# Output projection of a two-layer hybrid decoder trunk: which two mixers are summed first, in what order the projections are made, and how fast the background work is issued

## The chip, the cores and the metric

The kernel runs on one core of one Trainium2 chip. The metric is the device time of one execution in microseconds (us). Before the change it is 1254.05 us, the median of 3 runs (1253.93 to 1257.28).

## The reference

All data is f32; x is 512 tokens by 1024 channels. Each of two layers first makes four mixers of 256 channels out of one projection of the normed x, then sums them through one output projection, and ends with a SwiGLU feed-forward:

```python
for l in range(2):
    mod = silu(c) @ ada_w[l] + ada_b[l]            # six vectors of 1024
    sh1, sc1, g1, sh2, sc2, g2 = split(mod, 6)
    h = rmsnorm(x, norm_mix_g[l]) * (1 + sc1) + sh1
    fq, fk, fv, ff, pu, rq, rk, rv, rg, cu = split(h @ w_in[l])
    y_fox  = fox_attention(fq, fk, fv, ff, fox_fb[l])   # 4 heads x 64, causal, forget gate
    y_pool = pool_mixer(pu, pool_w[l], pool_scale[l])   # running means over 2, 4, 8, 16
    y_ret  = retention(rq, rk, rv, rg, gn_g[l])         # 4 heads x 64, chunks of 128, head norm, gate
    y_conv = conformer_conv(cu, ...)                    # GLU, depthwise k=31, layernorm, swish
    mix = concat([y_fox, y_pool, y_ret, y_conv])
    x = x + g1 * (mix @ w_out[l])
    h = rmsnorm(x, norm_ffn_g[l]) * (1 + sc2) + sh2
    x = x + g2 * ((silu(h @ w1[l]) * (h @ w3[l])) @ w2[l])
return rmsnorm(x, final_g)
```

## The kernel before

Activations lie channel by token: a tile is 128 channels by 512 tokens, so x is eight tiles `xT` and each mixer is two. `mix[0..7]` are, in this order, fox 0 and 1, pool 0 and 1, ret 0 and 1, conv 0 and 1.

**Products.** Every f32 product is three passes of TensorE (PE) over halves of the operands, a rounded part and a rest: L265 rounded by rounded, L266 rest of the data by rounded weight, L267 rounded data by rest of the weight. A weight tile comes by DMA (`raw`, mostly 512 KB), ScalarE (ACT) makes its rounded part `wh` (L164) and VectorE (DVE) the rest `wl` (L169). Activations are split likewise (`ah` L479 on ACT, `al` L480 on DVE; `yh` L438 and `yl` L442 for the normed x). There are 3 PSUM banks `mm` for products, 4 called `sm` and one `aux`, and 4 pairs `wh`/`wl`.

**Background work.** What isn't a big product is written as generators that are advanced a step at a time in `slot()`, which the main code calls after each product; each has a rate (`r_...` in layer 0, `q_...` in layer 1). They are: `ada`/`adaV`, which multiplies the ada_w rows by silu(c) on DVE (L318, L320; here called acs steps; a 256 KB DMA each into 3 buffers `ada`, with a small POOL copy L659 ahead of each load, and a set of 8 steps gives 512 of the 6144 columns); `conv` (30 multiply-adds for each of two tiles at L740, then a tail: column sums on PE L746, L748, squares L751 and L753, L404, L416, the power on POOL L408, back over the partitions L424, L758 to L761, split); `fox` (L812 to L850); `ret` for the pairs of heads 0 and 1 (scores L905, L911, states L922 to L930, sums L939 and L944, then the head norm: ACT L947, PE L951, DVE L416, POOL L408, DVE L957, PE L961, DVE L963, split L479/L480); and `pool` (L983 to L997). `finish_bg` runs a generator to its end at that place of the program. A scheduler may still move instructions of different generators past each other; each engine then works off its own list in order.

**Order of the main code.** After the fox and conv projections come those named in the table `MO`: `pu` (pool), `rk`, `rq`, `rv`, `rg` (gate of retention, L1136 and L1137, whose tile `hp` has 2 buffers that the conv taps also use) and four `o`. An `o` is a quarter of part 1 of the output projection: two of the eight output tiles, over four of the eight mixer tiles, added to `xT` through L1052. Before the change part 1 sums pool and conv. Part 2 sums fox and ret: three tiles with the mixer outermost, in the order `OB`, then five tiles in two halves of 256 tokens. The second norm follows (L404, L408, L424, L429, L438), and then the feed-forward in three segments of 8, 7 and 7 hidden tiles; a gated tile is L1232 on DVE, then L479/L480. During the feed-forward of layer 0 `adaV` makes the last vector of layer 0 and five of layer 1.

## Time and profile before

| | |
|---|---|
| median of 3 runs | 1254.05 us |
| the profiled execution | 1255.27 us |
| its span, first to last instruction | 1253.5 us |
| PE busy | 1209.0 us, 96% |
| DVE busy | 761.2 us, 61% |
| ACT busy | 406.5 us, 32% |
| POOL busy | 95.5 us, 8% |
| mean granted PE clock | 0.974 |
| HBM read | 154.74 MB |

A line of the page's groups gives the line of the kernel, engine and operation, what is written and read, how often, then busy time and mean ns of one, then the idle time of the engine just before. A line of the waits says which engine sat at which line for whom, the sum, how often, and the longest, all in us. A line of the timeline is start and duration, and in brackets idle time before it and what ended that. A line of the windows gives, for a stretch, each engine's busy time (and instructions), the granted PE clock, the DMA share and GB/s.

### The profile page before, as it was taken

What the parts mean: (1) busy time and instruction counts of PE and PEld (TensorE: products, weight loads), DVE (VectorE), ACT (ScalarE), POOL (GpSimd) and SP (SyncE); (2) the same over time, 40 slices, a digit from 0 to 9 for tenths busy, and PEclk for the clock granted to TensorE, in tenths of its full rate; (3) what the DMA queues carried; (4) which work ended last, traced back from release to release, by engine and by line L of the source; (5) the groups of instructions that cost most, each with busy time, mean ns of one, the idle gap of its engine ahead of it and who ended that gap; (6) DMA issues with size and microseconds to landing.
All of it is one profiled execution on the core that took longest, in us unless ns stands there. A gap on an engine that the chain in (4) does not pass through costs nothing.

```text
span 1253.5 us, 16762 instructions
## 1 busy us (share of the span) xinstructions
PE 1209.0 (96%) x6373; PEld 1004.1 (80%) x6373; DVE 761.2 (61%) x1332; ACT 406.5 (32%) x654; POOL 95.5 (8%) x186
## 2 busy tenths in 40 slices
PE   9999989999998999999999999899999999999997
PEld 8778666789876888888899886678988888888887
DVE  6799997577777555453357998457653333333333
ACT  5433334244322222123234244424432223213222
POOL 5432210102000000000000000000100000000000
PEclk8999978999998999999999999899999999999999
DMA  9766622226777545343233343022443323233321
GB/s 308 215 207 187 201 86 76 68 68 190 244 226 239 167 135 173 103 137 97 75 96 95 96 130 84 9 94 84 154 149 101 99 86 99 74 113 101 95 74 68
DMA packets 223721, 160.05 MB, mean 128 GB/s; under 512 B 8374, under 2 KB 198032, under 8 KB 223640
## 3 DMA queue, kind: packets, MB, share of 16 engines
q1 hardware_dynamic: 223464, 158.90, 42.7%
q8 instruction: 50, 0.82, 0.3%
q14 instruction: 31, 0.25, 0.1%
q10 hardware_dynamic: 176, 0.08, 0.0%
HBM read 154.74 MB, written 2.11 MB: 125 GB/s over the span
## 4 chain that ended last, share of the span: by engine, by line
PE 74%; DMA 5%; DVE 4%; issue 1%; ACT 1%; POOL 0%; DVEq 0%; ACTq 0%
PE mm L265 22%; PE mm L266 22%; PE mm L267 22%; DMA ada<-in_ada_w 4%; DVE acs L320 1%; PE sm L812 1%; PE sm L850 1%; PE sm L265 1%; PE sm L266 1%; PE sm L267 1%; DVE wl L169 1%; DMA raw<-in_ffn_w 1%; PE sm L838 1%; PE aux L404 0%; PE sm L961 0%
## 5 line engine op out<-in xcount | busy, mean ns | idle before, releaser
L164 ACT CAST wh<-raw 128x1024 fp32r<-128x1024 f32 (+3 forms) x196 | 198.8, 1015 | 592.4 <-PE mm L266 385.0
L266 PE MATMUL mm<-yl,wh 128*128 128x512 f32 (+1 forms) x984 | 373.1, 381 | 2.2 <-DVE yl L442 2.1
L265 PE MATMUL mm<-yh,wh 128*128 128x512 f32 (+1 forms) x984 | 369.5, 382 | 5.2 <-ACT yh L438 5.2
L267 PE MATMUL mm<-yh,wl 128*128 128x512 f32 (+1 forms) x984 | 372.1, 379 | 0.0
L169 DVE TENSOR_TENSOR wl<-raw,wh 128x1024 fp32r<-128x1024 f32 (+3 forms) x196 | 231.7, 1183 | 137.8 <-ACT wh L164 131.2
L266 PEld LDWEIGHTS mm<-yl,wh 128*128 128x128 f32 x984 | 188.1, 191 | 38.6 <-DVE yl L442 3.5
L265 PEld LDWEIGHTS mm<-yh,wh 128*128 128x128 f32 x984 | 185.4, 191 | 40.6 <-ACT yh L438 6.2
L267 PEld LDWEIGHTS mm<-yh,wl 128*128 128x128 f32 x984 | 188.0, 191 | 36.3 <-issue 0.2
L265 PE MATMUL mm<-ah,wh 128*128 128x512 f32 (+1 forms) x516 | 189.4, 370 | 6.2 <-ACT ah L479 6.2
L266 PE MATMUL mm<-al,wh 128*128 128x512 f32 (+1 forms) x516 | 189.8, 368 | 0.8 <-DVE al L480 0.8
L267 PE MATMUL mm<-ah,wl 128*128 128x512 f32 (+1 forms) x516 | 188.7, 367 | 0.0
L320 DVE SCALAR_TENSOR_TENSOR acs<-ada,cact,acs 128x512 f32<-128x512 f32 x140 | 104.8, 748 | 42.6 <-DMA ada<-in_ada_w 40.4
L1052 DVE SCALAR_TENSOR_TENSOR xT<-mm,mod,xT 128x512 f32<-128x512 f32 (+1 forms) x86 | 57.7, 675 | 117.1 <-PE mm L267 116.8
L265 PEld LDWEIGHTS mm<-ah,wh 128*128 128x128 f32 x516 | 97.3, 189 | 24.0 <-ACT ah L479 6.8
L266 PEld LDWEIGHTS mm<-al,wh 128*128 128x128 f32 x516 | 97.6, 189 | 17.7 <-DVE al L480 1.2
L267 PEld LDWEIGHTS mm<-ah,wl 128*128 128x128 f32 x516 | 97.6, 189 | 17.1 <-issue 0.2
L1232 DVE TENSOR_TENSOR t<-t,mm 128x512 f32<-128x512 f32 x42 | 28.8, 685 | 100.5 <-PE mm L267 100.5
L740 DVE SCALAR_TENSOR_TENSOR hc<-hp,cwT,hc 128x512 f32<-128x512 f32 x120 | 85.3, 745 | 1.0 <-ACT hc L737 0.9
L408 POOL TENSOR_TENSOR r<-r,mhalf 128x2 f32<-128x2 f32 (+3 forms) x16 | 18.1, 1133 | 535.3 <-DVE r L416 535.3
L659 POOL COPY ada<-yl 128x1 f32<-128x1 f32 x80 | 42.0, 531 | 153.7 <-DVE acs L320 103.1
L265 PE MATMUL mm<-wh,yh 128*128 128x256 f32 (+1 forms) x128 | 39.4, 308 | 2.7 <-DVE v L1124 2.7
L438 ACT ACTIVATE yh<-t,mod 128x256 fp32r<-128x256 f32 (+1 forms) x56 | 27.9, 533 | 35.6 <-DVE t L429 27.7
(257 smaller groups left out, 1176.2 us busy)
## 6 DMA issues: line engine op xcount, KB each, us to landing
raw<-in_ffn_w SPq DMA_DIRECT2D x104, 512.0 KB, 4.2
ada<-in_ada_w SPq DMA_DIRECT2D x160, 256.0 KB, 3.4
raw<-in_w_in SPq DMA_DIRECT2D x32, 512.0 KB, 4.2
raw<-in_ffn_w SPq DMA_DIRECT2D x32, 448.0 KB, 3.6
ad<-in_ada_w SPq DMA_DIRECT2D x32, 256.0 KB, 5.9
raw<-in_w_out SPq DMA_DIRECT2D x32, 256.0 KB, 3.1
raw<-in_w_in SPq DMA_DIRECT2D x4, 520.0 KB, 4.4
xn<-in_x SPq DMA_DIRECT2D x4, 512.0 KB, 6.4
```

The lines of the kernel that those rows point to most:

```text
L164: A.copy(h[:, 0:n], raw)
L169: V.tensor_tensor(out=lo[:, 0:n], in0=raw, in1=f(h[:, 0:n]), op=ALU.subtract)
L265: PE.matmul(o, lh, rh, start=start, stop=False)
L266: PE.matmul(o, lh, rl, start=False, stop=False)
L267: PE.matmul(o, ll, rh, start=False, stop=stop)
L320: V.scalar_tensor_tensor(out=acc, in0=r, scalar=ck, in1=acc, op0=ALU.mult, op1=ALU.add)
L408: G.tensor_tensor(out=out_, in0=ms, in1=mhalf[:, 0:ms.shape[-1]], op=ALU.pow)
L438: A.activation(yh[k][:, u:v], y, AF.Identity, bias=shift(l, i, k), scale=1.0)
L659: G.tensor_copy(t_[:, 0:1], f(yl[k][:, at:at + 1]))
L740: V.scalar_tensor_tensor(out=hcs[j], in0=hps[j][:, t:t + S], scalar=cwT[:, l, j, t:t + 1], in1=hcs[j], op0=ALU.mult, op1=ALU.add)
L1052: V.scalar_tensor_tensor(out=xT[:, n, u:v], in0=b[:, u:v], scalar=mod[l][:, gcol + n:gcol + n + 1], in1=xT[:, n, u:v], op0=ALU.mult, op1=A ...
L1232: V.tensor_tensor(out=t_, in0=t_, in1=b3, op=ALU.mult)
```

## The change

Part 1 of the output projection now sums fox and ret (order `OA`: fox 0, ret 0, fox 1, ret 1), part 2 pool and conv. Before part 1 the program finishes retention and fox instead of pool and conv; pool is finished at the first tile of part 2, conv at its third. While part 1 runs, `conv` and `ada` take their rates from a new table `LATE` (2.0 each). In both layers the projections come as `rk rq rv rg pu`, so the gate of retention is made ahead of part 1; layer 1 made it between the third and the fourth `o` before. The rates also change, and `FB` (layer 0) goes from 1 to 2.

```diff
-... 'MO': 'pu rk rq rg rv o o o o', 'MO1': 'pu rk rv rq o o o rg o', ... 'FB': 1, 'FB1': 2, ... 'r_ada': 0.6, 'r_conv': 0.7, 'r_fox': 0.85, ... 'r_adaV': 0.4, 'q_conv': 1, ... 'OA': (1, 0, 2, 3), 'OA1': (0, 1, 3, 2), 'OB': (1, 2, 0, 3), 'OB1': (1, 3, 0, 2), ...
+... 'MO': 'rk rq rv rg pu o o o o', 'MO1': 'rk rq rv rg pu o o o o', ... 'FB': 2, 'FB1': 2, ... 'r_ada': 0.45, 'r_conv': 0.65, 'r_fox': 1.2, ... 'r_adaV': 0.7, 'q_conv': 0.65, ... 'OA': (0, 2, 1, 3), 'OA1': (0, 2, 1, 3), 'OB': (0, 1, 2, 3), 'OB1': (0, 1, 2, 3), ...
+LATE = dict(conv=2.0, ada=2.0)
...
             if n == "o":
-                plan.append(wout(l, outs, 1))
+                plan.append(wout(l, outs, 0))
...
-        plan += [wout(l, i, 0) for i in range(4)]
+        plan += [wout(l, i, 1) for i in range(4)]
...
     def slot(w=1.0):
         for e in list(running):
-            e[1] += RATE[cur["layer"]][e[0]] * w * cur["on"]
+            r = LATE.get(e[0]) if cur["part"] else None
+            e[1] += (r or RATE[cur["layer"]][e[0]]) * w * cur["on"]
...
         def do_o():
             if not outs:
-                finish_bg(pg)
-                finish_bg([cg])
+                finish_bg(rgens)
+                finish_bg([fg])
+                cur["part"] = 1
...
-                    prod_out(b, h, lo, c, q, (2, 3, 6, 7)[q], 0, S, q == qs[0], q == qs[-1])
+                    prod_out(b, h, lo, c, q, (0, 1, 4, 5)[q], 0, S, q == qs[0], q == qs[-1])
...
             if q == 0:
-                finish_bg([fg])
+                finish_bg(pg)
             if q == 2:
-                finish_bg(rgens)
+                finish_bg([cg])
             for i in range(N1):
-                prod_out(banks[i], *tile_of(i), i, q, (0, 1, 4, 5)[q], 0, S, q == qs[0], q == qs[-1])
+                prod_out(banks[i], *tile_of(i), i, q, (2, 3, 6, 7)[q], 0, S, q == qs[0], q == qs[-1])
```

The same exchange of mixer tiles stands in the two loops of part 2 that follow. Line numbers of the changed kernel are higher by 2 to 5 (L740 becomes L743, L320 L323, L1052 L1055, L1232 L1237).

On VectorE in layer 0, the last steps of the second pair of heads (`qk_438` is its tile, `r8` its variances, `xT_93` the residual, `wl` the rest of a weight tile) stood before among evictions of the output projection:

```order
L957 SCALAR_TENSOR_TENSOR qk_438_2334<-sm_426_2259,vecH_120,hp_332_1747 128x512
L1052 SCALAR_TENSOR_TENSOR xT_93<-mm_428_2276,mod0_110,xT_93 128x512
L169 TENSOR_TENSOR wl_431_2294<-raw_429_2289,wh_430_2292 128x1024
L1052 SCALAR_TENSOR_TENSOR xT_93<-mm_435_2312,mod0_110,xT_93 128x512
L416 TENSOR_SCALAR r8_434_2309<-aux_121 128x8
L1052 SCALAR_TENSOR_TENSOR xT_93<-mm_442_2350,mod0_110,xT_93 128x512
L169 TENSOR_TENSOR wl_445_2368<-raw_443_2363,wh_444_2366 128x1024
L963 TENSOR_TENSOR qk_438_2334<-qk_438_2334,sm_439_2336 128x512
L480 TENSOR_TENSOR al_441_2347<-qk_438_2334,ah_440_2346 128x512
```

Now the same steps (`qk_382`) come ahead of every eviction, and the acs steps (`acs_458`) of the adaLN vectors lie between them:

```order
L419 TENSOR_SCALAR r8_377_1996<-aux_121 128x8
L316 TENSOR_TENSOR mod0_110<-aux_121,adbT_118 128x4
L321 TENSOR_SCALAR acs_458_2426<-ada_459_2427,cact_117 128x512
L323 SCALAR_TENSOR_TENSOR acs_458_2426<-ada_460_2431,cact_117,acs_458_2426 128x512
L323 SCALAR_TENSOR_TENSOR acs_458_2426<-ada_461_2444,cact_117,acs_458_2426 128x512
L316 TENSOR_TENSOR mod0_110<-aux_121,adbT_118 128x4
L323 SCALAR_TENSOR_TENSOR acs_458_2426<-ada_462_2448,cact_117,acs_458_2426 128x512
L323 SCALAR_TENSOR_TENSOR acs_458_2426<-ada_463_2452,cact_117,acs_458_2426 128x512
L966 TENSOR_TENSOR qk_382_2021<-qk_382_2021,sm_383_2023 128x512
L323 SCALAR_TENSOR_TENSOR acs_458_2426<-ada_464_2456,cact_117,acs_458_2426 128x512
L323 SCALAR_TENSOR_TENSOR acs_458_2426<-ada_465_2469,cact_117,acs_458_2426 128x512
L483 TENSOR_TENSOR al_385_2034<-qk_382_2021,ah_384_2033 128x512
```

The variance step and the product with it (L416 and L963, now L419 and L966) were two evictions and a weight split apart; now five acs steps lie between them, and two more ahead of the split of the result.

On TensorE in layer 1, the spreading of the head norm (L961; `r8_1301` are its variances) stood before inside a run of output projection products:

```order
L266 MATMUL mm_1311_7385<-al_1118_6393,wh_1272_7170 128x512
L267 MATMUL mm_1311_7385<-ah_1117_6392,wl_1273_7172 128x512
L265 MATMUL mm_1311_7385<-ah_1171_6617,wh_1272_7170 128x512
L266 MATMUL mm_1311_7385<-al_1172_6618,wh_1272_7170 128x512
L961 MATMUL sm_1307_7357<-ident_74,r8_1301_7330 64x128 x8
L267 MATMUL mm_1311_7385<-ah_1171_6617,wl_1273_7172 128x512
L265 MATMUL mm_1311_7385<-ah_1262_7102,wh_1272_7170 128x512
L266 MATMUL mm_1311_7385<-al_1263_7103,wh_1272_7170 128x512
L267 MATMUL mm_1311_7385<-ah_1262_7102,wl_1273_7172 128x512
```

Now the sums over the heads (L947), the variances (L954) and their spreading (L964) follow each other, and after one product of the pooling come the first products that read the split result (`ah_1262`):

```order
L947 MATMUL sm_1253_7024<-qk_1163_6567,st_1247_6991 64x128 x2
L947 MATMUL sm_1253_7024<-qk_1163_6567,st_1248_6993 64x128 x2
L947 MATMUL sm_1253_7024<-qk_1163_6567,st_1249_6995 64x128 x2
L954 MATMUL aux_121<-hones_82,t_1254_7039 128x2 x4
L964 MATMUL sm_1261_7074<-ident_74,r8_1255_7045 64x128 x8
L1000 MATMUL sm_1276_7173<-pl_1274_7163,pw_1273_7159 128x512
L268 MATMUL mm_1280_7183<-ah_1262_7084,wh_1229_6919 128x512
L268 MATMUL mm_1281_7201<-ah_1262_7084,wh_1229_6919 128x512
L268 MATMUL mm_1288_7244<-ah_1262_7084,wh_1257_7063 128x512
```

In the first list products stand on both sides of L961, 29 of them since its variances; in the second none stands between the three steps.

On VectorE at the start of the feed-forward of layer 0, between the first and the second gated tile (L1232, `mm_511` and `sm_513` are their gates), four acs steps stood before:

```order
L1232 TENSOR_TENSOR t_536_3000<-t_536_3000,mm_511_2741 128x512
L320 SCALAR_TENSOR_TENSOR acs_554_3084<-ada_584_3260,cact_117,acs_554_3084 128x512
L169 TENSOR_TENSOR wl_529_2938<-raw_527_2934,wh_528_2936 128x1024
L320 SCALAR_TENSOR_TENSOR acs_554_3084<-ada_585_3264,cact_117,acs_554_3084 128x512
L480 TENSOR_TENSOR al_538_3004<-t_536_3000,ah_537_3003 128x512
L381 STREAM_TRANSPOSE acs_586_3268<-acs_554_3084 128x512
L318 TENSOR_SCALAR acs_598_3340<-ada_599_3341,cact_117 128x512
L169 TENSOR_TENSOR wl_532_2968<-raw_530_2964,wh_531_2966 128x1024
L382 TENSOR_REDUCE ared_553_3083<-acs_586_3268 128x16
L320 SCALAR_TENSOR_TENSOR acs_598_3340<-ada_600_3345,cact_117,acs_598_3340 128x512
L1232 TENSOR_TENSOR t_539_3007<-t_539_3007,sm_513_2743 128x512
```

Now, between the first and the second (L1237), one stands, and another behind the second:

```order
L1237 TENSOR_TENSOR t_536_3000<-t_536_3000,mm_511_2741 128x512
L171 TENSOR_TENSOR wl_529_2938<-raw_527_2934,wh_528_2936 128x1024
L323 SCALAR_TENSOR_TENSOR acs_548_3059<-ada_572_3178,cact_117,acs_548_3059 128x512
L483 TENSOR_TENSOR al_538_3004<-t_536_3000,ah_537_3003 128x512
L1237 TENSOR_TENSOR t_539_3007<-t_539_3007,sm_513_2743 128x512
L323 SCALAR_TENSOR_TENSOR acs_548_3059<-ada_573_3182,cact_117,acs_548_3059 128x512
```

The second gated tile has moved ahead of three acs steps.

9 lines of the change are left out of this document (5 added, 4 removed).

## The prediction

> **What bounds the kernel now.** I read the page's busy times first, then the list of what PE waited for, then windows over the two stretches that the change rewrites, and last the timeline inside them.
>
> ```profile
> span 1253.5 us, 16762 instructions
> PE 1209.0 (96%) x6373; PEld 1004.1 (80%) x6373; DVE 761.2 (61%) x1332; ACT 406.5 (32%) x654; POOL 95.5 (8%) x186
> PE mm L265 <- ACT ah L479: 6.2, 2, 5.8
> PE mm L265 <- ACT yh L438: 5.2, 4, 1.8
> PE aux L404 <- DVE t L753: 2.8, 2, 2.0
> PE sm L424 <- POOL r L408: 2.5, 2, 1.3
> ```
>
> PE is the bound; 1253.5 − 1209.0 = 44.5 us is all that its idle time can give back, besides time at a reduced clock. The change keeps PE's products, so it can only move waits and clock losses. Windows of the stretches that it touches (length, then busy time of PE, PEld, DVE, ACT, POOL, the granted clock, DMA share, GB/s):
>
> ```profile
> 150.00:160.00 10.00, 6.12 (x43) 4.68 (x42) 9.97 (x25) 1.87 (x7) 1.92 (x5) 0.99 0.52 157
> 160.00:170.00 10.00, 9.04 (x47) 6.50 (x47) 10.00 (x28) 2.89 (x8) 1.48 (x3) 0.84 0.29 83
> 170.00:180.00 10.00, 8.97 (x46) 7.10 (x46) 10.00 (x23) 3.76 (x8) 1.22 (x3) 0.66 0.22 67
> 180.00:190.00 10.00, 7.92 (x57) 5.95 (x54) 9.96 (x35) 4.31 (x11) 0.76 (x2) 0.83 0.22 67
> 200.00:210.00 10.00, 7.36 (x53) 5.31 (x52) 5.63 (x20) 3.49 (x8) 1.02 (x1) 0.88 0.01 2
> 210.00:220.00 10.00, 9.23 (x72) 7.59 (x73) 8.90 (x16) 5.84 (x10) 1.76 (x7) 0.78 0.42 131
> 680.00:780.00 100.00, 100.00 (x571) 81.87 (x571) 91.19 (x192) 43.15 (x78) 0.56 (x5) 1.00 0.42 115
> 790.00:800.00 10.00, 9.23 (x91) 6.85 (x89) 4.16 (x9) 3.64 (x8) 0.00 (x0) 1.00 0.01 2
> 800.00:810.00 10.00, 7.80 (x50) 6.89 (x49) 2.78 (x6) 3.13 (x6) 3.02 (x2) 0.66 0.00 0
> ```
>
> In layer 0 DVE is full from 150 to 190 while PE isn't: DVE sets the pace there. In layer 1 PE is full from 680 to 780, and then chains of small steps starve it, 800 to 810 worst.
>
> **Layer 0, up to the second norm.** The order of the changed program shows that all 60 conv taps still lie ahead of the first product of part 1, as before. What really moves beside the output projection is the conv tail. Between the first tap and the second step of the retention gate DVE now has 24 acs steps where it had 32, 14 weight rests where it had 12, and one pool tile where it had two.
>
> ```profile
> L740 DVE SCALAR_TENSOR_TENSOR hc<-hp,cwT,hc 128x512 f32<-128x512 f32 x120 | 85.3, 745 | 1.0 <-ACT hc L737 0.9
> L320 DVE SCALAR_TENSOR_TENSOR acs<-ada,cact,acs 128x512 f32<-128x512 f32 x140 | 104.8, 748 | 42.6 <-DMA ada<-in_ada_w 40.4
> L169 DVE TENSOR_TENSOR wl<-raw,wh 128x1024 fp32r<-128x1024 f32 x152 | 185.7, 1222 | 108.2 <-ACT wh L164 102.4 <-PE mm L267 0.6
> L983 DVE TENSOR_TENSOR pl<-pl 128x512 f32<-128x512 f32 x8 | 5.5, 687 | 0.7 <-PE sm L997 0.7
> 188.72 0.68 DVE L1137 SCALAR_TENSOR_TENSOR hp<-hp,mm 128x512 f32<-128x512 f32 x1
> 206.75 1.07 PE L404 MATMUL aux<-ones,t 128*128 128x1 f32 x8 [1.96 <-DVE t L753]
> 270.96 0.50 PE L404 MATMUL aux<-ones,P 128*128 128x1 f32 x4
> ```
>
> That is 8 × 0.748 = 6.0 less, 2 × 1.222 = 2.4 more, and a pool tile of five to six steps of L983's size, 3.5 to 4, less: about 7.5 us. The gate's second step ends at 189.4 before, so at about 182 now. This gain is real only if it survives the chain behind it. Ahead of part 1 now stand the rest of fox and both pairs of retention. Fox needed 14 us from the gate to its last DVE step in the trace (about 189 to 203), so it ends at 195 to 196. From there DVE's list has 15 acs steps ahead of the last split of retention, and the DMA of their rows sets their pace:
>
> ```profile
> 210.66 1.60 DVE L320 SCALAR_TENSOR_TENSOR acs<-ada,cact,acs 128x512 f32<-128x512 f32 x2
> 219.72 0.75 DVE L320 SCALAR_TENSOR_TENSOR acs<-ada,cact,acs 128x512 f32<-128x512 f32 x1
> 385.20 0.39 PE L267 MATMUL mm<-ah,wl 128*128 128x512 f32 x1
> 385.43 0.39 PE L265 MATMUL mm<-ah,wh 128*128 128x512 f32 x1
> ```
>
> The two of the first row and the five up to the last are seven steps, so 219.72 − 210.66 = 9.06 us for six starts, 1.5 each. Three are loaded ahead, so 12 × 1.5 = 18 us, plus some 4 to 5 for the steps of the chain that lie between: the second pair is ready at about 218 (bounds: 214.5 if the ring of buffers never holds the chain, 222 if each acs step does). What is queued behind a late acs step on DVE is the retention chain itself, and PE waits for that.
>
> The last two rows give the cost of a 512-column product from start to start, 0.23 us (0.2335 over long runs). The output projection is 8 tiles × 24 = 192 of these; by the order PE can issue only 27 of them before the second pair is ready. So 165 × 0.2335 = 38.5 us are left at 218, with about 7 us of small matmuls (the conv tail's sums and spreads, pooling, adaLN sums). The conv tail keeps its own wait: 1.96 us in the trace, since the first step reads the squares of L753; 2 to 3 now. One clock drop costs about 2.5 (below), evictions and the last halves 1.5. 218 + 38.5 + 7 + 2.8 + 2.5 + 1.5 = 270.3, against 270.96 for the norm's first sum: **−1 us**, bounds −5 to +4 by those of 218. So the lead of 7.5 us is spent: pool and conv products used to cover the second pair of heads, and nothing covers it now.
>
> **Layer 1.** Here DVE isn't the bound ahead of part 1, so fewer acs steps save nothing. The 48 products of `rg` are now ahead of part 1 and cover nothing behind it: 48 × 0.2335 = 11.2 us. Before, they and part 1 hid the second pair's chain, whose steps the first pair shows:
>
> ```profile
> 798.86 0.60 ACT L947 ACTIVATE t<-sm 128x512 f32<-128x512 f32 x1 [3.36 <-PE sm L944]
> 799.51 1.05 PE L951 MATMUL aux<-hones,t 128*128 128x2 f32 x8 [0.70 <-ACT t L947]
> 800.60 0.17 DVE L416 TENSOR_SCALAR r<-aux 128x8 f32<-128x8 f32 x1 [1.26 <-PE aux L951]
> 800.84 2.02 POOL L408 TENSOR_TENSOR r<-r,mhalf 128x8 f32<-128x8 f32 x1 [43.23 <-DVE r L416]
> 806.53 1.98 PE L961 MATMUL sm<-ident,r 128*64 128x128 f32 x16
> 810.53 0.61 ACT L479 CAST ah<-hc 128x512 fp32r<-128x512 f32 x1
> 865.53 0.50 PE L404 MATMUL aux<-ones,P 128*128 128x1 f32 x4
> 869.07 0.61 PE L424 MATMUL sm<-ident,r 128*128 128x128 f32 x4
> ```
>
> From the end of the sums, 798.8, to the end of the power, 802.86, PE has only L951's 1.05 us to do, so 3 us are idle if nothing covers them; behind L961 come its product on DVE (0.7) and the split (0.6), 1.3 more, of which one pooling product takes about 0.7. So about 4 us lie bare. Fox ended at about 795 before; with 11.2 us of gate products ahead, some idle time filled, it ends at about 805 now. Ret pair 1 follows: 13.2 us of its chain (scores, states, sums, the norm, the split) and 4.2 us for 18 products that fit in, so ready at 822.4. Then 165 × 0.2335 = 38.5 and 5.4 us of small ones, 3.3 for the conv tail's waits (the longest of L404, 2.0, and of L424, 1.3), 1.2 for the power of the norm (the other wait of L424), 2.5 of clock: 873.3 for L424, against 869.07: **+4 us**, bounds +1 (the wait is filled by pool products) to +8 (a second clock drop).
>
> **Feed-forward of layer 0.** Its first segment is paced by acs steps, and the longest wait of the kernel ends it:
>
> ```profile
> 290.81 0.49 DVE L318 TENSOR_SCALAR acs<-ada,cact 128x512 f32<-128x512 f32 x1 [1.34 <-DMA ada<-in_ada_w]
> 378.99 0.68 DVE L1232 TENSOR_TENSOR t<-t,mm 128x512 f32<-128x512 f32 x1
> 380.38 0.80 PE L265 MATMUL mm<-ah,wh 128*128 128x512 f32 x1 [5.80 <-ACT ah L479]
> 432.62 0.69 DVE L1232 TENSOR_TENSOR t<-t,mm 128x512 f32<-128x512 f32 x1 [0.81 <-PE mm L267]
> 378.00:379.00 1.00, 0.00 (x0) 0.00 (x0) 0.96 (x3) 0.00 (x0) 0.00 (x0) 0.66 1.02 293
> 384.00:385.00 1.00, 1.00 (x4) 0.81 (x3) 0.96 (x2) 0.00 (x0) 0.00 (x0) 0.50 0.39 139
> ```
>
> Before the eighth gated tile (378.99) lie 52 acs steps in the order of before, 50 now: (378.99 − 290.81) / 52 = 1.70 us each. Two fewer are 3.4 us off a wait of 5.8: **−3 us**. Bounds: −6 if the tile also misses the clock drop, +2 because 31 acs steps instead of 20 now follow up to the ninth tile: 81 × 1.73 + 290.8 = 431, where 432.62 is its start before. So that tile would become just late; two spare banks, 11 us of products, stand between it and PE, and I take no loss.
>
> The last two rows price a clock drop. The clock falls at 378.7, some 4 us after PE fell idle, and stays at 0.50 until 385.1, so 4.7 us of products from 380.4 run at half speed: 2.4 us lost.
>
> **A rule beside it.** Between 800 and 810 the clock falls too (0.66 on average), with PE busy 7.80 of 10 us though the waits on L753 and L408 that the list has for this place are at most 2.0 and 1.3 us. The Trainium skill, "TensorE: Matmul & The Clock Gate", Part 1 (What's actually happening), has the clock drop after at least one idle window of about 3.4 us. The first drop agrees with that, the second doesn't. By the rule alone the shortened wait at the eighth tile costs no clock, and the sum would be 2.4 us lower; the row of 800 says that it may, and I go by the row.
>
> **The sum.** −1 + 4 − 3 = 0 us on the profiled execution's 1255.27 (span 1253.5 and 1.8 around it). That execution lies 1.2 above the median, so on the median's scale 1254.05 + 0, rounded **1254.0**. Ends: −5 + 1 − 6 = −10 and 4 + 8 + 2 = +14, so 1244 to 1268. A measurement can tell about 0.3%, 3.8 us: same is 1250.3 to 1257.8.
>
> **The rivals.**
>
> Faster: layer 0's lead of 7.5 us survives because the ring of ada buffers doesn't hold up the retention chain (ready at 214.5, −4.5), and the 5.8 us wait vanishes with its clock drop (−6); layer 1 costs +2. Sum −8 or so: 1246. For it: DVE full from 150 to 190, so any unloading counts. Against it: DMA idle ahead of 15 of the acs steps ends most of L320's idle time (40.4 of 42.6 us). Chance 0.30.
>
> Slower: the bare chain of the second pair decides. In both layers PE stands through the power (2.02 us on POOL) and the split, the clock drops, and the conv tail, now late, brings its own wait and a second drop: layer 0 +3, layer 1 +7, feed-forward 0 because the 31 acs steps behind the eighth tile eat the gain. Sum +10: 1264. It decides from the point where fewer than some 12 products are left to issue when pair 1's sums end. The order of layer 1 speaks for it, with none there; against it the three-bank start of part 2, which may be reordered. Chance 0.32.
>
> The change doesn't do what it says: conv is no more beside the output projection than before, since its taps still end ahead; what is left is an exchange of which pair of mixers is late, 1254 ± 2. Chance 0.08.
>
> No clock drop at short waits: 5.8 − 3.4 = 2.4 us are left at the eighth tile, and if the clock holds there, the 2.4 us of its drop go too: 1251.6. For it speaks that the drop of 378.7 came only after 4 us of idle time; against it 800 to 810. Chance 0.06. With the forecast's own 0.24 (1251 to 1257) these two make up "same", 0.38.
>
> The range reaches from the faster case to just beyond the slower: **1244 to 1266**, leaving out the far end of the slower case.
>
> **What would show it.** Right: the gate's second step at about 182; the second pair's split at about 218 in layer 0 and 822 in layer 1 with a wait of PE on it, clock near 0.6 to 0.7 there; norm sum at about 270; the wait at the eighth gated tile between 2 and 3.5 us, the ninth tile near 431. Wrong: no wait of PE on the second pair's split, or retention ready long before 214 in layer 0; a conv tail that PE waits for 5 us or more; new waits of PE on evictions or gated tiles between 380 and 450.

## The result, and the profile after

The changed kernel takes **1270.09 us**, the median of 4 runs (1267.94 to 1272.79), against 1255.66 for the kernel before, run beside it (1253.93 to 1261.36): a ratio of 1.0108 with a 95% interval of 1.0067 to 1.0149. Measured a second time, again beside the kernel before, it gave 1270.73 us and 1.0106 (1.0090 to 1.0122). So it is slower by 13 to 14 us, about 1%, and 1270 lies outside the range of 1244 to 1266.

The profiled execution took 1268.93 us. The page's first lines, and then some of the longest waits of PE (sum, times, longest):

```profile
span 1267.1 us, 16773 instructions
PE 1213.3 (96%) x6373; PEld 1004.5 (79%) x6373; DVE 760.8 (60%) x1332; ACT 408.8 (32%) x654; POOL 91.2 (7%) x186
```

```profile
PE mm L268 <- ACT ah L482: 12.7, 6, 6.8
PE mm L268 <- ACT yh L441: 7.5, 4, 2.8
PE sm L427 <- POOL r L411: 2.9, 3, 1.3
PE sm L964 <- POOL r L411: 2.0, 1, 2.0
```

PE has the same 6373 instructions but is busy 4.3 us longer (1213.3 − 1209.0), which no product explains: a busy PE at a lower clock counts as busy. Its idle time grew by 9.3 us (53.8 against 44.5). The waits for a split result (L482, before L479) doubled, from 6.2 to 12.7 us. For places in the program that both kernels have, the same instruction's start in both traces gives the loss by stretch (the norm sums are those of the timelines; "norm of layer 1" is the first column sum of its first norm). The changed kernel has a second profile, from its second measurement:

| stretch | before | after | after, second profile | differences | forecast |
|---|---|---|---|---|---|
| start to the first sum of the second norm, layer 0 | 270.96 | 277.33 | 276.39 | +6.4, +5.4 | −1 |
| from there to the norm of layer 1 | 378.42 | 383.55 | 382.72 | +5.1, +4.3 | −3 |
| from there to the 23rd gated tile of all (layer 1) | 247.54 | 250.72 | 253.51 | +3.2, +6.0 | +4 |
| from there to the end | 356.6 | 355.5 | 355.9 | −1.1, −0.7 | 0 |

So the same kernel differs by up to 2.8 us in one stretch from one execution to the next, and a difference of that size between two single profiles proves little.

**Layer 0 up to the norm.** The same windows as before, and those that follow (length, busy time of PE, PEld, DVE, ACT, POOL, granted clock, DMA share, GB/s):

```profile
150.00:160.00 10.00, 10.00 (x49) 7.12 (x47) 10.00 (x18) 2.17 (x5) 2.88 (x3) 1.00 0.45 142
160.00:170.00 10.00, 8.85 (x30) 5.49 (x30) 9.97 (x32) 3.49 (x8) 0.34 (x3) 0.83 0.40 131
170.00:180.00 10.00, 8.33 (x56) 5.82 (x53) 9.97 (x25) 6.05 (x15) 0.11 (x1) 1.00 0.14 45
180.00:190.00 10.00, 8.76 (x42) 5.21 (x43) 7.52 (x35) 4.71 (x14) 0.00 (x0) 0.83 0.03 11
200.00:210.00 10.00, 9.09 (x91) 7.49 (x91) 6.49 (x13) 2.52 (x5) 3.31 (x5) 1.00 0.25 81
210.00:220.00 10.00, 8.73 (x70) 7.36 (x70) 5.80 (x13) 0.60 (x1) 2.99 (x9) 0.91 0.45 141
220.00:230.00 10.00, 8.31 (x25) 4.79 (x22) 7.58 (x12) 2.87 (x4) 0.82 (x6) 0.50 0.40 125
230.00:240.00 10.00, 10.00 (x41) 8.01 (x41) 7.74 (x13) 2.62 (x3) 0.33 (x3) 0.91 0.32 105
```

DVE is full up to 180 and no longer after 180: the unloading worked. But from 220 to 230 PE gets 25 matmuls done in 8.31 us that are called busy, at clock 0.50. The timeline shows what it does there:

```profile
181.96 1.28 DVE L1141 SCALAR_TENSOR_TENSOR hp<-hp,mm 128x512 f32<-128x512 f32 x2
196.60 0.49 DVE L832 TENSOR_SCALAR P<-P,mx 128x512 f32<-128x512 f32 x1
202.57 0.69 DVE L483 TENSOR_TENSOR al<-sm,ah 128x512 fp32r<-128x512 f32 x1 [1.48 <-ACT ah L482]
203.25 0.48 DVE L321 TENSOR_SCALAR acs<-ada,cact 128x512 f32<-128x512 f32 x1
216.53 1.68 POOL L411 TENSOR_TENSOR r<-r,mhalf 128x8 f32<-128x8 f32 x1 [0.42 <-DVE r L419]
217.82 1.53 PE L379 MATMUL aux<-ones,acs 128*128 128x1 f32 x8 [0.25 <-DVE mod L316]
219.28 1.97 PE L964 MATMUL sm<-ident,r 128*64 128x128 f32 x16
221.18 2.08 PE L1000 MATMUL sm<-pl,pw 128*128 128x512 f32 x2
224.27 1.65 PE L268 MATMUL mm<-ah,wh 128*128 128x512 f32 x3 [1.02 <-ACT ah L482]
225.85 0.69 DVE L483 TENSOR_TENSOR al<-qk,ah 128x512 fp32r<-128x512 f32 x1
226.59 0.80 PE L269 MATMUL mm<-al,wh 128*128 128x512 f32 x1 [0.67 <-DVE al L483]
277.33 0.50 PE L407 MATMUL aux<-ones,P 128*128 128x1 f32 x4
287.95 0.50 PE L407 MATMUL aux<-ones,P 128*128 128x1 f32 x4
```

The gate ends at 183.2 and fox's last softmax step (L832) stands at 196.6, close to the forecast's 182 and 195 to 196. Fox's output is split only at 202.57, and the acs steps begin right behind it. The second pair of retention is split at 225.85, not at 218. What runs on PE in its bare chain are sums of one or two columns and the spreads (L954, L379, L964), at half clock from 218 on. From the split the 51.5 us to the norm's first sum are nearly what the forecast had (52.3).

This shows where layer 0 loses. The second pair is the last input of part 1 now. Before, the last input was the second conv tile, split here:

```profile
220.38 0.68 DVE L480 TENSOR_TENSOR al<-hc,ah 128x512 fp32r<-128x512 f32 x1
```

The norm's first sum came 50.6 us behind that (270.96 − 220.38), so 5.5 of the 6.4 us lie ahead of the last input and 0.9 behind it.

**Feed-forward of layer 0.** The last two rows of the timeline above are the two halves of the norm: 10.6 us lie between them, where before it was 4.8 (270.96 and 275.77). The trace has 35 matmuls of PE between the two sums now, most of them products of the feed-forward, and had 7 before. The first acs step and the eighth gated tile follow:

```profile
299.68 0.48 DVE L321 TENSOR_SCALAR acs<-ada,cact 128x512 f32<-128x512 f32 x1 [1.35 <-DMA ada<-in_ada_w]
390.88 0.68 DVE L1237 TENSOR_TENSOR t<-t,mm 128x512 f32<-128x512 f32 x1
392.27 0.79 PE L268 MATMUL mm<-ah,wh 128*128 128x512 f32 x1 [6.77 <-ACT ah L482]
448.86 0.68 DVE L1237 TENSOR_TENSOR t<-t,mm 128x512 f32<-128x512 f32 x1
```

The acs steps start 22.4 us behind the norm's first sum (before 19.9), and the 50 of them take 1.82 us each (91.2 / 50), not 1.70. So the eighth tile comes 113.6 us behind that sum instead of 108.0, and PE waits 6.8 us instead of 5.8.

**Layer 1.** The windows of its bare chain, and two rows of the timeline inside it:

```profile
820.00:830.00 10.00, 7.33 (x56) 5.72 (x57) 1.62 (x6) 0.60 (x1) 1.64 (x1) 0.96 0.15 54
830.00:840.00 10.00, 9.37 (x44) 6.47 (x41) 7.33 (x11) 4.05 (x6) 0.45 (x4) 0.87 0.00 0
```

```profile
829.62 1.98 PE L964 MATMUL sm<-ident,r 128*64 128x128 f32 x16 [1.97 <-POOL r L411]
833.02 0.69 DVE L483 TENSOR_TENSOR al<-qk,ah 128x512 fp32r<-128x512 f32 x1 [0.68 <-ACT ah L482]
```

Layer 1 begins 11.5 us later (660.88 against 649.38), so the forecast's 822.4 for the second pair becomes 833.9; it is 833.02.

### The profile page after: what moved, and what is told of

Same layout as the page of the kernel before. It is cut to its first block, busy times and chain, and to the rows that moved or that the text cites. A ratio compares the mean times of both kernels' runs of the same rounds, so it can differ in the third digit from the quotient of the medians.

```text
span 1267.1 us, 16773 instructions
## 1 busy us (share of the span) xinstructions
PE 1213.3 (96%) x6373; PEld 1004.5 (79%) x6373; DVE 760.8 (60%) x1332; ACT 408.8 (32%) x654; POOL 91.2 (7%) x186
## 4 chain that ended last, share of the span: by engine, by line
PE 72%; DVE 6%; DMA 5%; issue 2%; ACT 1%; POOL 1%; DVEq 0%; POOLq 0%; ACTq 0%
PE mm L269 21%; PE mm L268 21%; PE mm L270 21%; DMA ada<-in_ada_w 4%; DVE acs L323 2%; DVE wl L171 1%; PE sm L853 1%; PE sm L815 1%; DVE hc L743 1%; PE sm L268 1%; PE sm L269 1%; PE sm L270 1%; PE sm L841 1%; DMA raw<-in_ffn_w 1%; DVE al L483 0%
## 5 line engine op out<-in xcount | busy, mean ns | idle before, releaser
L268 PE MATMUL mm<-ah,wh 128*128 128x512 f32 (+1 forms) x516 | 189.6, 374 | 15.3 <-ACT ah L482 12.7
L269 PE MATMUL mm<-al,wh 128*128 128x512 f32 (+1 forms) x516 | 192.4, 373 | 1.6 <-DVE al L483 1.6
L270 PE MATMUL mm<-ah,wl 128*128 128x512 f32 (+1 forms) x516 | 192.0, 372 | 0.0
L323 DVE SCALAR_TENSOR_TENSOR acs<-ada,cact,acs 128x512 f32<-128x512 f32 x140 | 104.8, 749 | 47.2 <-DMA ada<-in_ada_w 44.9
L1055 DVE SCALAR_TENSOR_TENSOR xT<-mm,mod,xT 128x512 f32<-128x512 f32 (+1 forms) x86 | 57.2, 674 | 116.1 <-PE mm L270 116.1
L269 PEld LDWEIGHTS mm<-al,wh 128*128 128x128 f32 x516 | 98.7, 191 | 20.3 <-DVE al L483 2.7
L270 PEld LDWEIGHTS mm<-ah,wl 128*128 128x128 f32 x516 | 99.1, 192 | 17.3 <-issue 0.5
L1237 DVE TENSOR_TENSOR t<-t,mm 128x512 f32<-128x512 f32 x42 | 28.8, 685 | 98.3 <-PE mm L270 98.3
L743 DVE SCALAR_TENSOR_TENSOR hc<-hp,cwT,hc 128x512 f32<-128x512 f32 x120 | 85.6, 746 | 1.0 <-ACT hc L740 0.9
L411 POOL TENSOR_TENSOR r<-r,mhalf 128x2 f32<-128x2 f32 (+3 forms) x16 | 17.3, 1080 | 488.2 <-DVE r L419 488.2
L662 POOL COPY ada<-yl 128x1 f32<-128x1 f32 x80 | 38.3, 484 | 147.7 <-DVE acs L323 108.8
```

The costliest lines, as they stand in the source:

```text
L268: PE.matmul(o, lh, rh, start=start, stop=False)
L269: PE.matmul(o, lh, rl, start=False, stop=False)
L270: PE.matmul(o, ll, rh, start=False, stop=stop)
L323: V.scalar_tensor_tensor(out=acc, in0=r, scalar=ck, in1=acc, op0=ALU.mult, op1=ALU.add)
L411: G.tensor_tensor(out=out_, in0=ms, in1=mhalf[:, 0:ms.shape[-1]], op=ALU.pow)
L662: G.tensor_copy(t_[:, 0:1], f(yl[k][:, at:at + 1]))
```

## The experiments

After the result the theory was: the loss has separate parts, a late and bare chain of the second pair in layer 0, a second half of the norm that comes late and so delays the feed-forward's acs steps, and the chain of layer 1. The rivals: that the new rates of the background work cost it, above all the acs steps (`LATE`, `r_adaV`), that the second wait at the eighth tile only moves loss about, and, later, that the clock and not the wait is what costs in the bare chain. The letters A, B and C of the expectations are given anew in each of them.

### Which part of the change costs

The exchange of mixers alone, with the old rates and no late rates:

```diff
 (changed kernel)
-... 'FB': 2, ... 'r_ada': 0.45, 'r_conv': 0.65, 'r_fox': 1.2, ... 'r_adaV': 0.7, 'q_conv': 0.65, ...
+... 'FB': 1, ... 'r_ada': 0.6, 'r_conv': 0.7, 'r_fox': 0.85, ... 'r_adaV': 0.4, 'q_conv': 1, ...
-LATE = dict(conv=2.0, ada=2.0)
+LATE = dict()
```

> The changed kernel with all rates and FB as before and no late rates: fox and retention first, gate of retention ahead of part 1, pool and conv second. Theory A (the exchange itself costs, by the bare chain of the second pair in both layers): 1262 to 1268, norm sum of layer 1 still 4 us later relative to the layer's start. Rival B (the rates are what costs): within 3 us of the kernel before.

The new rates alone, on the kernel before (the diff's right-hand rates and `FB`, no exchange):

> The kernel before with the new rates and FB alone (no late rates, mixers in the old order). Theory A (the rates cost through the acs steps that they leave for the retention chain; with the old order they find cover): within 4 us of the kernel before, either side. Rival B (the new rates cost by themselves, by what they delay ahead of the output projection): 1262 or more.

Measured: the exchange alone 1264.39 us, ratio 1.0054 (1.0039 to 1.0069), the rates alone 1264.50 us, ratio 1.0055 (1.0036 to 1.0074). Each costs about 7 us, and the two add up to what the whole change costs. The prediction had taken the rates for harmless by themselves; they aren't. What PE waits for longest with the rates alone, from 150 to 300, and where:

```profile
PE sm L838 <- DVE P L829: 7.2, 2, 7.0
```

```profile
173.42 1.90 PE L838 MATMUL sm<-ident,P 128*128 128x128 f32 x6 [6.95 <-DVE P L829]
```

Fox, advanced faster, has its transposes (L838) next on PE's list, and PE stands 7 us for a softmax that DVE, full there, hasn't made. Part of that comes back; the norm's first sum is 3.5 us late (274.45), its second sum 9.7 us behind that. With the exchange alone the first sum is 2.4 us late (273.31), the second 10.9 behind, and the wait at the eighth tile 8.8 us. Each part by itself pushes the second half of the norm back, and each delays the last input of part 1: its split comes at 221.5 with the exchange alone (fox) and at 222.4 with the rates alone (conv), where it was 220.4 and is 225.9 with both. But the changed kernel, which has both parts, doesn't have the 7 us wait of PE for that softmax: its list of waits from 150 to 300 has none for a `P`. So that the costs add up doesn't show that they are the same costs.

### The acs steps in part 1

`LATE` advances the acs steps quickly while part 1 runs. Held back there:

```diff
-LATE = dict(conv=2.0, ada=2.0)
+LATE = dict(conv=2.0, ada=0.05)
```

> The changed kernel, with the rate of ada while part 1 runs at 0.05 instead of 2.0, so that the last set of acs steps lies behind the second pair's split on VectorE in layer 0 instead of ahead of it. Theory A (the acs steps, paced by their DMA, hold up the bare retention chain): some 7 acs steps fewer ahead of the split, at 1.5 us each; the products on the second pair start 6 to 10 us sooner than 224.3, the norm's first sum comes at 268 to 272 instead of 277.3, and the time falls by 5 to 8 us to about 1263. Rival B (the chain itself, through the power on GpSimd and the matmuls of the head norm, sets the point): the start moves by less than 2 us and the time stays within 2 us of 1270.

Measured: 1265.76 us, ratio 1.0081 (1.0049 to 1.0113). Its profiled run was the longest of its four (1273.76; the others 1264.65 to 1265.90), so the times of day in that trace are not compared. Within the chain, fox's split to the second pair's split took 18.6 us (206.8 to 225.4), 4.7 less than the 23.3 of the changed kernel. The median is some 4 us lower than the changed kernel's, between what the two theories gave, but the intervals overlap.

With a set of acs steps made ahead of the chain instead (rate of `ada` 0.8, then held back):

```diff
-... 'r_ada': 0.45, ...
+... 'r_ada': 0.8, ...
-LATE = dict(conv=2.0, ada=2.0)
+LATE = dict(conv=2.0, ada=0.05)
```

> The changed kernel with r_ada 0.8 and the late rate of ada at 0.05: the acs steps lie among the conv taps again, none between the steps of the two pairs of retention. Theory A (layer 0 has so much VectorE work in any order; steps taken out of the chain come back ahead of it): second step of the gate at 188 to 192 instead of 183, second pair's split at 220 to 226, norm sum at 273 to 278, time within 4 us of the changed kernel. Rival B (only the place in the chain costs): norm sum at 266 to 270, 1261 or less.

Measured: 1269.53 us, ratio 1.0090 (1.0057 to 1.0123). The chain takes 17.3 us from fox's split, but the gate now ends at 192.8 and fox's split comes at 208.0: the second pair is split at 225.3, the same. The DVE time that is taken out of the chain comes back ahead of it. And without a single acs step in it the chain is still 17.3 us long.

With six of the eight steps left out of each of two sets, 12 acs steps in all (so these two kernels leave out a part of one adaLN vector's sum), in the changed kernel and in the kernel before:

```diff
-                for k in range(KD):
+                for k in range(2 if on_pe and part == 4 else KD):
```

> The changed kernel, leaving out 12 of the 16 acs steps (with their 256 KB loads) of the two sets that lie inside the retention chain of layer 0; so a part of the sums for one adaLN vector is left out. Up to the first step of the retention gate all is as in the changed kernel. Theory A (paced by their loads, these steps hold the second pair): the product on the second pair's split starts at 214 to 218 instead of 224.3, the norm's first sum comes at 266 to 270 instead of 277.3, time 1260 to 1264. Rival B (the chain's own steps, the power on GpSimd and the clock drop set the point): start at 221 or later, time 1267 or more.

> The kernel before with the same 12 steps left out. By the order VectorE is freed of 6 steps ahead of the retention gate and 6 behind. In this order of the program the second sums of the norm also stand some 49 rows behind the first on TensorE (5 in the kernel before) and the second gated tile stands ahead of the acs steps, as in the changed kernel. Theory A (the late second half of the norm and the start of the acs steps behind it are what costs in the feed-forward, with either order of the mixers): from the norm's first sum to the first acs step 22 us or more (19.85 before), wait at the eighth gated tile 6.5 to 9 us, from the first sum to the norm of layer 1 381 to 384 us (378.4 before), while the first sum comes 4 to 8 us sooner; sum 1250 to 1256. Rival B (the feed-forward only shifts): 378 to 379 us there, and 1247 to 1250.

Measured: the changed kernel 1263.92 us, ratio 1.0059 (1.0034 to 1.0084), with a profiled run at 1270.94, above its median; in that trace the second pair is still split at 227.7. The kernel before 1251.75 us, ratio 0.9957 (0.9944 to 0.9970). By the medians the 12 steps are thus worth about 6 us to either kernel (1270.09 − 1263.92, and 1257.86 − 1251.75 for the kernel before measured beside it), and without them the two still lie 12.2 us apart. So these steps are not what makes the changed kernel the slower one. In the kernel before, the norm's first sum is 6.5 us earlier, but its second sum comes 9.6 us behind it instead of 4.8, and the stretch from the first sum to the norm of layer 1 takes 382.7 us instead of 378.4:

```profile
264.45 0.50 PE L404 MATMUL aux<-ones,P 128*128 128x1 f32 x4
274.03 0.50 PE L404 MATMUL aux<-ones,P 128*128 128x1 f32 x4
286.82 0.49 DVE L318 TENSOR_SCALAR acs<-ada,cact 128x512 f32<-128x512 f32 x1 [1.45 <-DMA ada<-in_ada_w]
```

So a late second half of the norm and 4 us more in the feed-forward occur together with the old order of mixers too. That the one makes the other isn't shown. In two of the runs below (4 fillers behind the second pair, and fox last) the second sum comes 10.8 and 11.1 us behind the first, and yet the stretch takes only 379.6 and 379.8 us. What all runs with late second sums share is the later start of the acs steps, 22.2 us or more behind the first sum instead of 19.9.

### The wait at the eighth tile

Rate of `adaV` back to 0.4 in the changed kernel, and up to 0.7 in the kernel before:

```diff
-... 'r_adaV': 0.7, ...      (changed kernel)
+... 'r_adaV': 0.4, ...
-... 'r_adaV': 0.4, ...      (kernel before)
+... 'r_adaV': 0.7, ...
```

> The changed kernel with r_adaV back at 0.4. The acs steps up to the eighth gated tile of layer 0 are nearly those of the changed kernel (51 instead of 50), and 21 instead of 31 follow up to the ninth. Theory A (the higher rate is what costs 5 us in the feed-forward of layer 0): the wait at the eighth gated tile falls from 6.8 to under 3 us and the time falls by 4 to 5 us to 1265. Rival B (the pace up to the eighth tile is set by the order in which the feed-forward starts, whatever the rate): the wait stays at 6 to 8 us and the time within 2 us of 1270.

> The kernel before with r_adaV at 0.7 and nothing else changed; acs steps up to the eighth gated tile 52 as before, then 29 instead of 20 up to the ninth. Theory A (the rate costs): 1259 to 1261, 4 to 5 us more than before, with new waits of TensorE between 380 and 450. Rival B (the rate costs nothing by itself): within 2 us of the kernel before.

Measured: 1271.94 us, ratio 1.0122 (1.0105 to 1.0139), with 9.0 us at the eighth tile; and 1254.51 us, ratio 0.9981 (0.9967 to 0.9994). This rate isn't what the change lost by.

Then the acs loads of layer 1's vectors were tied to the latest gated tile (one POOL copy of a column ahead of each load), so that the steps can't run ahead of the tiles; in the changed kernel, in the kernel before, and in the latter with a rate of 0.9:

```diff
+        elif l == 1:
+            G.tensor_copy(r[:, 0:1], f(glu8[0][:, 0:1]))
...
+                glu8[:] = [pr[1]]
```

> The changed kernel, in which the row loads of the acs steps for layer 1 wait (by the small GpSimd copy ahead of each) for the latest gated tile of the feed-forward, so that only 16 acs steps lie ahead of the eighth gated tile of layer 0 instead of 50. Theory A (the feed-forward's loss of 5 us comes from these steps and their loads): no wait over 1 us at the seventh and eighth gated tile (2.1 and 6.8 now), no clock drop there, 10 to 12 us less than the changed kernel, about 1259; what is left above the kernel before is the loss of the two mixers, and compared with the same edit to the kernel before it is 7 to 9 us slower instead of 14. Rival B (the feed-forward waits for its weight tiles, whatever the acs steps do): the wait at the eighth tile stays over 4 us and the time within 3 us of 1270.

> The kernel before with the same edit. Theory A: its wait of 5.8 us and the clock drop behind it (2.4 us) go, 1246 to 1249. Rival B: within 3 us of the kernel before.

> The kernel before, with the loads for layer 1 waiting for the latest gated tile and r_adaV 0.9 instead of 0.4, so that their steps end in time. Theory A (the wait at the eighth gated tile goes, and with the higher rate the 25.8 us at the adaLN sums of the run with 0.4 goes too): 1245 to 1250, faster than both kernels. Rival B (the waits at the adaLN sums take most of it back): 1252 to 1260.

Measured: 1266.03 us, ratio 1.0074 (1.0044 to 1.0103); 1284.33 us, ratio 1.0209 (1.0181 to 1.0238); and 1260.12 us, ratio 1.0022 (1.0008 to 1.0035). None comes out as its theory A had it (1259, 1246 to 1249, 1245 to 1250). The wait at the eighth tile is gone in all three: that tile starts at 376.6 instead of 390.9 in the changed kernel, at 369.9 and 368.1 instead of 379.0 in the kernel before. The waits on the column sums of the last vectors, in the changed kernel, then in the kernel before with rate 0.4 and 0.9 (each line from the trace of its own kernel):

```profile
PE sm L395 <- DVE ared L388: 5.3, 3, 2.9
```

```profile
PE sm L392 <- DVE ared L385: 25.8, 2, 23.4
```

```profile
PE sm L392 <- DVE ared L385: 9.5, 3, 4.8
```

The acs steps that are held back are due before layer 1 starts, and PE waits for them there. In the kernel before that takes back all that was gained and more. In the changed kernel it may not: the stretch from the norm's first sum to the norm of layer 1 falls from 383.6 to 378.8 us, and the median by 4.1 us, but the intervals overlap, so this stays open. These runs also isolate layer 0: without that wait in either, the eighth tile of the changed kernel is 6.7 us later (376.59 − 369.86), close to the 6.4 that were lost up to the norm.

### Layer 1 as before

Orders, mixers and `q_conv` of layer 1 put back, layer 0 left changed:

```diff
-... 'MO1': 'rk rq rv rg pu o o o o', ... 'q_conv': 0.65, ... 'OA1': (0, 2, 1, 3), ... 'OB1': (0, 1, 2, 3), ...
+... 'MO1': 'pu rk rv rq o o o rg o', ... 'q_conv': 1, ... 'OA1': (0, 1, 3, 2), ... 'OB1': (1, 3, 0, 2), ...
-                plan.append(wout(l, outs, 0))
+                plan.append(wout(l, outs, l))
...
-        plan += [wout(l, i, 1) for i in range(4)]
+        plan += [wout(l, i, 1 - l) for i in range(4)]
...
```

> The changed kernel with layer 1 as it was before (pool and conv first, gate of retention between the third and the fourth quarter of part 1, q_conv 1), layer 0 changed. Theory A (the bare chain of the second pair costs 3 to 5 us in layer 1, the rest of the loss lies in layer 0): 1265 to 1267. Rival B (the whole loss arises in layer 0 and its feed-forward, what layer 1 shows is a shift): within 1.5 us of the changed kernel, 1269 to 1272. Rival C (layer 1 carries most of it): under 1262.

Measured: 1272.32 us, ratio 1.0118 (1.0094 to 1.0142). Nothing comes back. In its trace the stretch from the norm of layer 1 to the 23rd gated tile takes 250.7 us, as in the first profile of the changed kernel, not 247.5. With the rates alone, where layer 1 has its old order, it takes 250.1. So layer 1 does lose some us, but its own order alone doesn't cause them; what of layer 0 carries over (the schedule as a whole is made anew for each kernel) stays open.

### Wait or clock

PE's waits in the bare chains filled with products whose result isn't used: identity times a 128x512 tile behind the variances of a pair (4) and in the conv tail (3 and 3); in the changed kernel for both pairs, in the kernel before for the first, which is the one that stands bare there:

```diff
+            dm = small()
+            for _ in range(4):
+                PE.matmul(dm, ident, sq, start=True, stop=True)
         r = token_rsqrt(pt, 8, 1.0 / 64)
...
```

> The changed kernel with extra matmuls of 512 columns that nobody reads: 4 behind the variances of each head norm, 3 behind the token sums and 3 behind the tanh of the conv tail, in both layers; some 6 us of extra work for TensorE in each layer, most of it in its waits. Theory C (the bare chains cost by the clock that their small matmuls let fall): clock loss up to the norm's first sum of layer 0 falls from 22.6 by 5 us or more, the stretch from 218 to 231 runs at full clock, the time falls to 1262 to 1266 in spite of the extra work. Rival B (the chains cost by their length): the clock loss stays within 2 us and the time rises by 2 to 6 us to 1272 to 1276.

> The kernel before with the same extra matmuls in the conv tail and behind the variances of the first pair only (the second is covered). Theory C: clock drops at 207 to 214 and 801 to 808 go, 1250 to 1254. Rival B: 1257 to 1261, later by the extra work that finds no wait.

Measured: 1283.32 us, ratio 1.0220 (1.0196 to 1.0245), and 1284.98 us, ratio 1.0241 (1.0216 to 1.0266). The doses were too large: each such f32 product runs as two passes, 0.43 us from start to start, and there are 28 of them in the changed kernel (6429 instructions of PE instead of 6373) and 20 in the kernel before. 28 of them lengthen the changed kernel by 13 us, about half of what they take, and 20 of them lengthen the kernel before by 30, more than the 17 that they take, so there the edit also moved other work (fox's second tile is split at 236.5 instead of 221.0). The clock of the changed kernel is 1.00 from 210 to 230 with the fillers. But by the measure that its expectation named, the clock loss up to the norm's first sum, 22.6 us became only 21.3, and neither theory's time was met.

So, in the changed kernel, only the 4 behind the second pair (3.7 us a layer), and then 2 of them (2.0 us a layer) beside the changed kernel itself on the same chip:

> The changed kernel with 4 extra matmuls behind the variances of the second pair's head norm only. Theory C: the drop that begins at 218 in layer 0 goes or is shorter, 2 to 5 us faster than the changed kernel. Rival B: no gain, 1270 to 1273.

> The changed kernel with 2 filler matmuls (1.9 us of TensorE per layer, of which nothing is used) behind the second pair's variances, half of the dose of the run with 4. Theory C (the bare chain's cost is mostly the clock drop behind it): clock near 1.00 at 218 to 231, 2 to 5 us below the changed kernel run beside it (1264 to 1268). Theory B (the clock is not what costs; the wait is): the same time as the changed kernel beside it, or up to 3.7 us above. Theory A (the late second half of the norm) says nothing here: the same time within 1 us.

> The changed kernel itself once more, so that the run beside it is compared on one chip at one time. Both theories: 1268 to 1272 us, ratio to before 1.009 to 1.013; in the profile the granted clock at 0.50 from about 218 to 231 us and the second pair's split near 225.

Measured: with 4 fillers 1267.85 us, ratio 1.0097 (1.0079 to 1.0116); with 2 fillers 1267.60 us, ratio 1.0080 (1.0062 to 1.0098); the changed kernel again 1270.73 us, ratio 1.0106 (1.0090 to 1.0122). With 2 fillers, 3.9 us of useless products in the two layers together, the kernel is 3.1 us shorter than the changed one beside it, within the 2 to 5 that the clock theory gave. The intervals still overlap (1.0062 to 1.0098 and 1.0090 to 1.0122), so the size isn't settled. What the clock does is plain in the windows, with 4 fillers:

```profile
210.00:220.00 10.00, 9.24 (x69) 6.37 (x69) 3.06 (x7) 0.60 (x1) 2.31 (x5) 1.00 0.34 108
220.00:230.00 10.00, 7.70 (x41) 5.38 (x36) 9.44 (x17) 2.93 (x5) 2.77 (x10) 1.00 0.43 134
```

and with 2:

```profile
210.00:220.00 10.00, 9.08 (x77) 6.86 (x75) 6.97 (x14) 1.35 (x3) 1.77 (x7) 1.00 0.53 165
220.00:230.00 10.00, 7.86 (x54) 5.51 (x51) 6.17 (x13) 2.31 (x4) 3.81 (x9) 1.00 0.41 125
```

The clock is 1.00 where the changed kernel has 0.50. The chain itself, fox's split to the second pair's, is 20.8 us with 2 fillers and 22.5 with 4, against 23.3 without (202.57 to 225.85; 23.3 again in the second profile). That the clock alone makes the chain shorter isn't shown: with the fillers the order changed as well, and 12 acs steps lie between the two splits instead of 15, since three of them and one group of single columns (L379) moved back. The mean clock of the six runs with 2 fillers is 0.974 to 0.979, that of the changed kernel's four 0.965 to 0.971.

Fox last instead (rate of `ret` up, of fox down), so that retention is ready before part 1:

```diff
-... 'r_fox': 1.2, 'r_ret': 1, ...
+... 'r_fox': 0.85, 'r_ret': 2, ...
```

> The changed kernel with r_ret 2 and r_fox 0.85: by the order both pairs of retention are split ahead of the second fox tile, which is last now. Theory C (whatever chain is last stands bare): the fox split comes at 218 to 226, the norm's first sum at 273 to 278, time within 4 us of the changed kernel. Rival B (the second pair of retention is the one that is too long): fox split by 214, norm sum at 270 or sooner, 1263 or less.

Measured: 1264.69 us, ratio 1.0082 (1.0059 to 1.0106). The second pair is split by 212.4 now, and fox's second tile at 226.3, half a microsecond after the retention of the changed kernel. Whichever chain is the last ahead of part 1 stands bare, with the clock at 0.74 from 210 to 230. The norm's first sum comes at 274.3, as theory C had it. The time lies 5.4 us below the changed kernel's, between the two theories, and the intervals overlap; so this order may be some us better, but it doesn't reach the kernel before. In that kernel the second pair is split at 251.1, in the middle of the output projection, and the pool and conv products stood beside its chain.

Of all these, none that does the whole work is below the kernel before by more than a measurement can tell; the nearest is the kernel before with `r_adaV` 0.7, at 0.9981.

## Why the prediction was wrong

**Layer 0, forecast −1, measured +6.4 (+5.4 in the second profile). The step that failed:** "Fox needed 14 us from the gate to its last DVE step in the trace (about 189 to 203), so it ends at 195 to 196. From there DVE's list has 15 acs steps ahead of the last split of retention". The 14 us were right for the last softmax step (196.6). But the acs steps don't stand behind that step; they stand behind the split of fox's output, and between the two lie transposes on PE, their copies on ACT, products with v, and the head norm of the first pair. The acs steps began at 203.25, so their start was 7 to 8 us off. From there the 15 steps and the chain took 22.6 us to the split at 225.85, where 18 plus 4 to 5 were forecast. That this part agrees is in part luck: the forecast took the acs steps for most of it, but in the run with the steps made ahead, none in the chain, it still is 23.3 us from the last softmax step to the second pair's split (202.0 to 225.3). With 15 it is 29.2. The bound "214.5 if the ring of buffers never holds the chain", 19 us behind fox's end, was too low by 4. In the kernel before, the same rows could have told: the last softmax step stands at 203.2 and the acs steps begin at 210.1. The second thing that the step missed is the clock inside the chain. The forecast had one drop at 2.5 us; by windows of 1 us (busy time times one minus the clock), 3.3 us were lost between gate and norm before and 8.1 now.

**What was right in it.** The gate's second step at 183.2 (182), DVE unloaded by some 6 us, 51.5 us from the second pair to the norm (52.3), the conv tail's wait of 1.9 us (2 to 3). The 51.5 hold 4.4 us of clock loss instead of 2.5, so other terms of that sum were too high by some 3 us together, and the agreement is in part luck. The gain of 6 us on DVE ended at the gate, as the text said it might.

**Feed-forward of layer 0, forecast −3, measured +5.1. The step that failed:** "Two fewer are 3.4 us off a wait of 5.8". There are two fewer (50 instead of 52). But both other factors were held as before: the start of the steps behind the norm's first sum (22.4 instead of 19.9 us, +2.5) and the pace (1.82 instead of 1.70, 50 times, +6.4). 2.5 + 6.4 − 3.4 = 5.5, which is the eighth tile's delay behind that sum (113.6 − 108.0). The late start goes along with the second sums, which moved back by 28 matmuls on PE; the prediction read only DVE's order there. The kernel before with fewer acs steps has the late sums and the late start without the change. The cause of the slower pace was not isolated, and it varies: 1.80 in the second profile of the changed kernel, 1.75 and 1.76 in the runs with fox last and with 4 fillers, which lose only about 1 us in this stretch.

**The ninth tile** was forecast "near 431" and "I take no loss"; it starts at 448.9, 16.2 us later than before, of which 11.9 are the eighth tile's delay and 4.3 lie between the two tiles, with the 31 acs steps there. From 300 to 460 PE's list of waits has only the 6.8 us above and 3.0 us for two gated tiles, so the ninth itself cost PE nothing that shows.

**Layer 1, forecast +4, measured +3.2 (+6.0 in the second profile).** Right in size and place: the second pair at 833.0 (833.9 after the shift), L964's wait on POOL of 2.0 us. Wrong in the clock there: 0.96 and 0.87, not 0.6 to 0.7. And putting layer 1 back returned nothing, so the number agrees better than the mechanism has been shown.

**The rivals.** The slower one had the mechanism: "The bare chain of the second pair decides", with the clock dropping and the feed-forward gaining nothing. It was priced at +3, +7 and 0, and the runs give +6.4, +3.2 and +5.1. Its condition, fewer than 12 products left to issue at the end of pair 1's sums, held in layer 0 too: of the 27 products that the forecast counted on, 9 went out from 185.9 to 191.0 and 18 from 206.6 to 212.6, all ahead of those sums' end (214.4), and none was left behind them. The faster rival fell: the acs steps do hold the chain (from fox's split 23.3 us with 15 of them, 17.3 to 20.3 with 8, 4 or none), but without them it is still long, and making them earlier moved the time ahead of the chain. "No clock drop at short waits" wasn't met, since the wait at the eighth tile got longer: the clock was 0.50 from 389 to 395.

**What no term had** is the rates. The prediction worked them into the counts of acs steps only, and the run with the rates alone shows a cost of 7 us by themselves. The wait that is its first sign, PE at fox's transposes, isn't there in the changed kernel, so by which path the rates cost in it stays open; what the runs show is a later last input of part 1 (222.4 with the rates alone, 220.4 before).

## What to carry to other kernels

When a chain is moved ahead of a stage, price it from the last instruction that its successor in the engine's list stands behind, which is a split or a copy on another engine and not the chain's last heavy step; the old trace has that gap. Look at the order on the engine that is the bound, too: here a reduction that moved back by 28 matmuls went along with a loop behind it that started 2.5 us later. And a background rate is part of the schedule: change it alone first, since it can cost as much as the structure that it was meant to serve.
